# Hybrid decoder trunk on one core: w_down products at other places among the Strassen products, and half of the compression copies on ScalarE

## The chip, the cores and the metric

The kernel runs on one core of a Trainium2 chip. A core has TensorE (matmuls, PE in the profile, and PEld for its weight loads), VectorE (DVE), ScalarE (ACT), GpSimd (POOL) and SyncE (SP, which here only issues transfers). The engines run side by side, each through its own list of instructions in a fixed order, and they wait for one another by semaphores. The metric is the device time of one execution in microseconds (us): 1538.51 us before, the median of 3 runs that lie between 1538.48 and 1538.63.

## The reference: what is computed

Two decoder layers on 512 tokens of width 1024 in float32. A layer normalises its input, projects it with `w_in`, runs two token mixers side by side (forgetting attention with 8 heads; sparse attention with 8 heads whose branches are compressed, selected and sliding-window), gates and mixes them, adds the result to the input, and ends with a squared-ReLU MLP:

```python
kc = compress_blocks(kc, cmp_pos[0], cmp_w1[0], cmp_b1[0], cmp_w2[0], cmp_b2[0])
vc = compress_blocks(vc, cmp_pos[1], cmp_w1[1], cmp_b1[1], cmp_w2[1], cmp_b2[1])
...
x = x + mixed @ w_out
h = rmsnorm(x, norm_mlp)
return x + jnp.square(jax.nn.relu(h @ w_up)) @ w_down
```

`compress_blocks` takes blocks of 32 tokens at a stride of 16 (31 blocks, which overlap by half), adds a position table, and sends each flattened block through two small matrices with a GELU between them. `w_up` is 1024x4096 and `w_down` 4096x1024. A final normalisation follows the second layer.

## The kernel before

**Numbers.** Every large product is made with float32 values split in two: a high half (a cast, `h` or `oh`) and a low half (the value minus the cast, `lo` or `ol`). A block of weights thus costs a cast on ACT and a subtraction on DVE (lines 186 and 187), and one product term costs three matmuls: high by high, high by low, low by high (lines 212, 213, 214).

**Compression.** `compress` (line 498) first lays the tokens of the key `kc` and the value `vc` out anew. For each of the two, two tiles `ca` are filled, one per half of the overlap, each with a memset (506), a copy of the position table (508) and four copies of 64x248 elements (511). That is 16 such copies in a layer, all on DVE. `compress` runs as filler work while the forgetting attention runs; `attend` (469) steps through scores, transposes and values and takes projections and compression between them. In the attention DVE reads the scores out of their bank and finds the row maximum (398, `mx`), ACT makes the exponential (399), PE transposes it into a bank `ps_PT` (421), ACT casts that bank (430, `pth`) and DVE subtracts (431, `ptl`), after which the bank is free for other transposes.

**The MLP.** `w_up` is 32 blocks of 128 columns. The first 8 (`PLAIN`) are plain products. The other 24 are taken in 12 pairs, and each pair is one unit of a Strassen scheme (`unit`, 1228): seven products, here P0 to P6, in place of eight. A Strassen product is 8 matmuls (line 1224): four of 512 columns with the high half of the weights and four of 256 with the low half. P0 goes into a bank `m`; ACT copies it (1245); P1 goes into a bank `p5`, which ACT copies too (1249); P2 is added onto `m`, which ACT copies again (1253); P3 has its own bank (1256); P4 is added onto `m`, and DVE adds the result to both halves of `z` (1260); P5 has its own bank, which DVE reads (1265); P6 is added onto `p5`, which DVE reads (1269). From `z` and then from `y` comes a block of activations each: `act` (1284) runs ReLU, square and a cast on ACT (1289, 1290, 1291) and the low half as a subtraction on POOL (1292). The operands of the next unit are made inside the unit as well (`convert`, 1195): seven casts on ACT, seven subtractions on DVE, and four sums, of which POOL makes two.

There are 32 blocks of activations, numbered 0 to 31: 0 to 7 from the plain products, then two from each unit (unit k, counted from 0, makes 8+2k and 9+2k). Their halves live in the buffers `oh` and `ol`, of which there are eight each, so block j takes the place of block j-8 when all who read that one are done. The tiles `y` and `z` live in four buffers `zz`.

**w_down in the gaps.** The first 24 blocks of activations are consumed in six groups of four. One w_down product takes one group and one of the 8 output blocks: 12 matmuls (lines 212 to 214), with a DVE addition onto the residual `x` behind them (949). That makes 48 products, d0 to d47 here, where d(8c) to d(8c+7) read group c, that is blocks 4c to 4c+3. d0 to d11 come before the units. The other 36 are spread over the 12 units by a list of counts (992). Inside a unit, `between` is called at four places: place 0 between P1 and P2, place 1 between P3 and P4, place 2 between P5 and P6, and place 3 behind P6. A unit with n products puts them at its first n places. With the counts 2, 2, 3, 3, 4, 4, 4, 4, 4, 4, 2, 0, d16 to d18 are in unit 2, d19 to d21 in unit 3, d42 to d45 in unit 9, d46 and d47 in unit 10, and unit 11 has none.

**The last eight blocks.** Activations 24 to 31 are consumed by 8 products of 24 matmuls (one per output block): in layer 0 with 512 columns, in layer 1 (`last`, 1013) in two halves of the tokens with 256 columns, where the seventh of eight terms of two blocks is followed by the eighth of both.

**Order.** The code names an order, but the order on each engine is fixed by a planner when the kernel is built: it takes instructions in the order of the code as far as their inputs and buffers are ready by its own estimate, and lets a later one pass where an earlier one is not. A changed instruction can therefore change the order of those around it. PSUM banks are given out in turn by `bank` (687), two under each of four names, one per product. Weights of w_down come by transfers on SP's queue into one buffer (`crs`) that is refilled when its block is converted; conversion of the next block is asked for inside the current product (`ahead`, 199 and 215).

Of the kernel before, what the change touches and what calls it, by code (L numbers as in the profile page):

```python
# [18 lines left out]
D = 1024  # L19
# [118 lines left out]
def run(*gens):  # L138
    for g in gens:
        for _ in g:  # L140
            pass


class Body:
# [353 lines left out]
    def compress(self, kc, vc, small, l):  # L498

        nc, a = self.nc, self.a  # L500
        A = []
        for x, pos in ((kc, "pos_k"), (vc, "pos_v")):
            t = [self.t("t2", [128, 8, 2, 32], name="ca") for _ in range(2)]
            v = x.rearrange("p (n j r) -> p r j n", j=8, r=2)
            for half in range(2):
                nc.vector.memset(t[half][:, :, 1, 31], 0.0)
                o = OFF[pos] + 8 * half
                nc.vector.tensor_copy(t[half][:, :, 0, 31], small[:, o:o + 8])
                for h in range(2):
                    for r in range(2):  # L510
                        nc.vector.tensor_copy(t[half][r * 64:(r + 1) * 64, :, h, :31],
                                              v[h * 64:(h + 1) * 64, r, :, half:half + 31])
            A.append(t)
            yield
        hp = self.p("O")
# [24 lines left out]
        h = self.t("tmp", [128, 256])  # L540
# [6 lines left out]
        g = self.t("tmp", [128, 4, 64], name="g")  # L547
# [35 lines left out]
        v = self.t("tmp", [128, 2, 64])  # L583
# [344 lines left out]
    def mlp(self, l, x, u, acc, gm):  # L928

        nc, a = self.nc, self.a  # L930
        R = None
        pend = []
        acts = []

        def act(ps):
            t = self.t("tmp", [128, T])
            nc.vector.scalar_tensor_tensor(t, ps, 0.0, R, op0=OP.max, op1=OP.mult)
            h = self.t("oh", [128, T], F32R)
            lo = self.t("ol", [128, T], F32R)
            nc.scalar.activation(t, t, AF.Square)  # L940
            nc.scalar.copy(h, t)
            nc.vector.tensor_tensor(lo, t, h.bitcast(F32), op=OP.subtract)
            acts.append((h, lo))

        def down(c, m, w):

            ps = self.bank()
            yield from self.gemm(ps, w, 4 * (m % 2), acts[4 * c:4 * c + 4], ks=4)
            nc.vector.tensor_add(x[m], x[m], ps)

        def downs():
            for c in range(6):
                for m in range(8):
                    if m % 2 == 0:
                        w = self.weights(a["wd2"][l, c, m // 2])
                    yield lambda: run(down(c, m, w))

        S = Strassen(self, l, x, gm)
        D = downs()
        raws = [None] * 16  # L960
        g0 = self.PLAIN // 2
        S.load(g0)
        for j in range(self.PLAIN):
            ps = self.bank()
            w = self.weights(a["wup"][l, j].rearrange("p k c -> p (k c)"))
            run(self.gemm(ps, w, 0, u))
            if R is None and j == 0:
                pend.append(ps)
                continue
            if R is None:  # L970
                R, _ = self.rstd(acc, (self.turn_tag(), self.turn_tag()))
                prep = S.prepare(R)
                for p in pend:
                    act(p)
            act(ps)
            for _ in range(3):
                next(prep, None)
        conv = S.convert(g0)
        for i in range(12):
            next(D)()  # L980
            if i < 7:
                next(prep, None)
                next(prep, None)
            elif i == 7:
                run(prep)
            else:
                next(conv, None)
                next(conv, None)
            if i == 10:
                S.load(g0 + 1)  # L990
        run(conv)
        for g, n in zip(range(g0, 16), (2, 2, 3, 3, 4, 4, 4, 4, 4, 4, 2, 0)):
            S.load(g + 2)
            S.unit(g, D, n, acts)
        u_next = []
        acts = acts[24:]
        if l + 1 < L:
            acc = []
            self.load_small(l + 1)
            for m in range(8):  # L1000
                ps = self.bank()
                w = self.weights(a["wdn"][l, m].rearrange("p k c -> p (k c)"))
                run(self.gemm(ps, w, 0, acts))
                nc.vector.tensor_add(x[m], x[m], ps)
                acc = self.sumsq(x[m], acc, m == 7)
                u_next.append(self.make_u(x[m], self.gain[:, 16 * l + 16:16 * l + 24], m))
                nc.scalar.dma_start(self.xs[m], x[m])
        else:
            self.last(x, acts, a["wdn"][l])
        self.acc = acc  # L1010
        return u_next
# [106 lines left out]
class Strassen:  # L1118
# [109 lines left out]
    def unit(self, g, D, n, acts):  # L1228
        b, nc = self.b, self.nc
        V, A = nc.vector, nc.scalar  # L1230
        conv = self.convert(g + 1)
        todo = iter(range(n))

        def between():
            if next(todo, None) is not None:
                next(D)()

        def product(i, onto=None):
            ps = b.bank() if onto is None else onto
            self.product(ps, g, i, onto is None)  # L1240
            return ps

        m = product(0)
        y = b.t("zz", [128, 2, 512], name="y")
        A.copy(y[:, 0], m)
        next(conv, None)
        p5 = product(1)
        z = b.t("zz", [128, 2, 512], name="z")
        A.copy(z[:, 1], p5)
        next(conv, None)  # L1250
        between()
        product(2, m)
        A.activation(y[:, 1], m, AF.Copy, scale=-1.0)
        next(conv, None)
        p4 = product(3)
        A.copy(z[:, 0], p4)
        next(conv, None)
        between()
        product(4, m)
        V.tensor_tensor(z, z, m[:, None, :].to_broadcast([128, 2, 512]), op=OP.add)  # L1260
        pair = [None, None]
        self.act(self.halves(z), pair, 0)
        next(conv, None)
        p2 = product(5)
        V.tensor_tensor(y[:, 0], p2, y[:, 0], op=OP.subtract)
        next(conv, None)
        between()
        product(6, p5)
        V.tensor_tensor(y[:, 1], y[:, 1], p5, op=OP.subtract)
        self.act(self.halves(y), pair, 1)  # L1270
        acts += pair
        next(conv, None)
        between()
        for _ in conv:
            pass
# [54 lines left out]
```

## Time and profile before

| what | value |
| --- | --- |
| median of 3 runs | 1538.51 us |
| the profiled execution, its own time | 1538.79 us |
| its span, first to last instruction | 1537.0 us |
| mean granted TensorE clock | 0.998 |
| PE busy | 1516.9 us (99%) |
| DVE busy | 1131.1 us (74%) |
| ACT busy | 808.0 us (53%) |
| POOL busy | 215.5 us (14%) |
| Strassen units of layer 0, of layer 1 | 500.5 to 720.6 us, 1258.2 to 1478.3 us |
| compression copies of layer 0, of layer 1 | from 81.3 us, from 838.9 us |

A row of a timeline gives the start in us, the duration in us, the engine, the line of the kernel, the operation, the tiles (out<-in) with their shapes, and how many instructions the row merges; in brackets behind it stands how long the engine had been idle before it and for whom it waited. Matmuls overlap: one of 512 columns is shown with some 0.40 us, but the next one starts 0.23 us later. Lost time on PE is therefore read from starts, not from durations. In a wait row stand the engine that waited, the instruction it waited for, the total in us, the number of times and the longest. A row of a stretch gives, behind its length, the busy us of PE, PEld, DVE, ACT and POOL.

### The profile page before, as it was taken

Reading aid. Unit: us, or ns where it says so; the run is one execution under the profiler, and the core shown is the slowest. Engines: PE = TensorE matmul, PEld = TensorE weight load, DVE = VectorE, ACT = ScalarE, POOL = GpSimd, SP = SyncE. Lnnn points to the kernel's source line nnn. Section 1 sums busy time; section 2 is a strip of 40 time slices with the busy share of each in tenths; the row PEclk is TensorE's granted clock in tenths of the full one; section 3 lists DMA queues with packets and bytes.
Section 4 is the critical chain, followed back from the end, with each engine's and each line's share of the span. In section 5 each row is a group of like instructions: output and inputs, shape, how many; then the busy total and the mean of one; then the engine's idle time right before and its main releaser. Section 6 shows DMA issues by size and latency. Waiting matters only on the chain.

```text
span 1537.0 us, 21391 instructions
## 1 busy us (share of the span) xinstructions
PE 1516.9 (99%) x7772; PEld 1270.3 (83%) x7772; DVE 1131.1 (74%) x2207; ACT 808.0 (53%) x1513; POOL 215.5 (14%) x178
## 2 busy tenths in 40 slices
PE   9999999999999999999999999999999999999997
PEld 8878888888888888888887788878888887888887
DVE  5588988867479877775646799887574989777753
ACT  6445665553454655555434556555434635655562
POOL 4000000000201332222300000000002023222222
PEclk9999999999999999999999999999999999999999
DMA  7545422143323322322546543222422233223121
GB/s 262 176 127 146 131 69 83 56 128 107 109 85 121 110 96 96 110 83 64 177 142 170 157 120 96 73 79 70 149 98 97 88 118 102 105 95 102 63 97 55
DMA packets 56633, 169.49 MB, mean 110 GB/s; under 512 B 7344, under 2 KB 8112, under 8 KB 56528
## 3 DMA queue, kind: packets, MB, share of 16 engines
q1 hardware_dynamic: 53072, 161.84, 33.2%
q10 hardware_dynamic: 3456, 6.29, 1.2%
q8 instruction: 61, 1.00, 0.3%
q14 instruction: 44, 0.36, 0.1%
HBM read 140.77 MB, written 4.19 MB: 94 GB/s over the span
## 4 chain that ended last, share of the span: by engine, by line
PE 92%; DVE 4%; ACT 1%; DMA 1%; issue 1%; POOL 1%; SPq 0%; DVEq 0%; POOLq 0%; ACTq 0%
PE ps_mm L212 12%; PE ps_mm L213 12%; PE ps_mm L214 12%; PE ps_O L1224 4%; PE ps_S L1224 4%; PE ps_O L447 4%; PE ps_PT L212 3%; PE ps_PT L213 3%; PE ps_PT L214 3%; PE ps_mm L1224 3%; PE ps_PT L1224 3%; PE ps_PT L421 3%; PE ps_S L212 2%; PE ps_S L213 2%; PE ps_S L214 2%; PE ps_O L212 2%
## 5 line engine op out<-in xcount | busy, mean ns | idle before, releaser
L186 ACT CAST wh<-raw 128x1024 fp32r<-128x1024 f32 (+2 forms) x187 | 192.4, 1029 | 254.0 <-PE ps_mm L213 63.1
L187 DVE TENSOR_TENSOR wl<-raw,wh 128x1024 fp32r<-128x1024 f32 (+2 forms) x187 | 227.8, 1218 | 52.4 <-ACT wh L186 51.1
L212 PE MATMUL ps_mm<-uh,wh 128*128 128x512 f32 x512 | 202.4, 395 | 0.0
L213 PE MATMUL ps_mm<-ul,wh 128*128 128x512 f32 x512 | 201.4, 393 | 0.0
L214 PE MATMUL ps_mm<-uh,wl 128*128 128x512 f32 x512 | 201.4, 393 | 0.0
L399 ACT ACTIVATE E<-E,mx 128x128 f32<-128x128 f32 x192 | 107.9, 562 | 75.2 <-DVE mx L398 72.4
L213 PE MATMUL ps_mm<-ol,wh 128*128 128x512 f32 (+1 forms) x324 | 126.1, 389 | 2.7 <-POOL ol L1292 2.7
L212 PE MATMUL ps_mm<-oh,wh 128*128 128x512 f32 (+1 forms) x324 | 126.2, 390 | 0.1
L214 PE MATMUL ps_mm<-oh,wl 128*128 128x512 f32 (+1 forms) x324 | 125.5, 387 | 0.0
L430 ACT CAST pth<-ps_PT 128x512 fp32r<-128x512 f32 x144 | 72.9, 511 | 86.3 <-PE ps_PT L421 86.1
L214 PEld LDWEIGHTS ps_mm<-uh,wl 128*128 128x128 f32 x512 | 96.2, 188 | 19.8
L212 PEld LDWEIGHTS ps_mm<-uh,wh 128*128 128x128 f32 x512 | 96.2, 188 | 18.3 <-ACT E L399 1.5
L1214 DVE TENSOR_TENSOR sl<-s,sh 128x512 fp32r<-128x512 f32 x96 | 85.9, 898 | 31.4 <-ACT sh L1213 30.9
L213 PEld LDWEIGHTS ps_mm<-ul,wh 128*128 128x128 f32 x512 | 96.6, 189 | 14.9
L398 DVE CUSTOM_DVE_ANT_0 E<-ps_S,ct 128x128 f32<-128x128 f32 x192 | 91.5, 480 | 21.6 <-PE ps_S L395 20.4
L431 DVE TENSOR_TENSOR ptl<-ps_PT,pth 128x512 fp32r<-128x512 f32 x144 | 85.3, 595 | 26.1 <-ACT pth L430 25.6
L253 POOL TENSOR_TENSOR acc<-sq 128x512 f32<-128x512 f32 (+1 forms) x6 | 8.6, 1435 | 579.0 <-DVE wl L187 566.0
L421 PE MATMUL ps_PT<-ct,E 128*128 128x128 f32 x480 | 84.3, 274 | 2.5 <-DVE ptl L431 2.5
L1213 ACT CAST sh<-raw 128x512 fp32r<-128x512 f32 x72 | 44.7, 620 | 73.9 <-PE ps_PT L1224 28.1
L1213 ACT CAST sh<-s 128x512 fp32r<-128x512 f32 x96 | 59.4, 619 | 40.3 <-PE ps_O L1224 14.8
L1214 DVE TENSOR_TENSOR sl<-raw,sh 128x512 fp32r<-128x512 f32 x72 | 59.4, 825 | 20.6 <-ACT sh L1213 20.6
L421 PEld LDWEIGHTS ps_PT<-ct,E 128*128 128x128 f32 x480 | 60.1, 140 | 17.1 <-DVE ptl L431 4.2
(420 smaller groups left out, 3948.5 us busy)
## 6 DMA issues: line engine op xcount, KB each, us to landing
raw<-wb SPq DMA_DIRECT2D x64, 512.0 KB, 4.7
raw<-wup SPq DMA_DIRECT2D x64, 512.0 KB, 3.5
raw<-wd SPq DMA_DIRECT2D x48, 512.0 KB, 3.5
kd<-hl SPq DMA_DIRECT2D x48, 256.0 KB, 4.9
w<-w SPq DMA_DIRECT2D x32, 256.0 KB, 4.4
q<-hl SPq DMA_DIRECT2D x64, 128.0 KB, 2.8
raw<-wo SPq DMA_DIRECT2D x16, 512.0 KB, 3.7
raw<-wout SPq DMA_DIRECT2D x16, 512.0 KB, 3.5
```

What stands on the lines that cost most here:

```text
L186: nc.scalar.copy(h[:, :n], raw[:, :n])
L187: nc.vector.tensor_tensor(lo[:, :n], raw[:, :n], h[:, :n].bitcast(F32), op=OP.subtract)
L212: mm(ps, h[:, c], xh, start=start and i == 0, stop=False)
L213: mm(ps, h[:, c], xl, start=False, stop=False)
L214: mm(ps, lo[:, c], xh, start=False, stop=stop and i == ks - 1)
L398: nc.vector.tensor_tensor_reduce(e, ps[:, :n], self.mask[:, T - n:], -1.0, BIG, OP.add, OP.min, mx)
L399: nc.scalar.activation(e, e, AF.Exp, bias=mx, scale=-1.0, accum_out=sm[:, i:i + 1])
L421: nc.tensor.transpose(ps[:, j * 128:(j + 1) * 128], E[i][:, b * 128:(b + 1) * 128], self.ident)
L431: nc.vector.tensor_sub(lo[:, o:o + n], ps[:, :n], h[:, o:o + n].bitcast(F32))
L1213: nc.scalar.copy(h, src)
L1214: nc.vector.tensor_tensor(lo, src, h.bitcast(F32), op=OP.subtract)
L1224: mm = lambda o, w, x, **kw: self.nc.tensor.matmul(o, w, x, skip_group_check=True, **kw)
```

## The change

It has three parts. In `compress`, of each tile's four copies of 64x248 the two that read the upper 64 partitions (`h` = 1) are issued on ACT, the other two stay on DVE: 8 of a layer's 16. In `unit`, the number n of w_down products picks a set of places: for n = 2 places 0 and 1 and for n = 4 all four, as before; for n = 3 places 1, 2 and 3 where it was 0, 1 and 2; for n = 1 place 1. In `mlp`, the counts of the last three units become 3, 1 and 0 where they were 4, 2 and 0, and the two products that are left run behind the last unit. So d16 to d21 and d42 to d44 each stand one place later (d42 to d44 at places 1, 2 and 3 of unit 9), d45 moves from place 3 of unit 9 to place 1 of unit 10, and d46 and d47 move from unit 10 to behind unit 11. The number of matmuls is the same.

```diff
                 for h in range(2):
                     for r in range(2):
-                        nc.vector.tensor_copy(t[half][r * 64:(r + 1) * 64, :, h, :31],
-                                              v[h * 64:(h + 1) * 64, r, :, half:half + 31])
+                        copy = nc.scalar.copy if h else nc.vector.tensor_copy
+                        copy(t[half][r * 64:(r + 1) * 64, :, h, :31], v[h * 64:(h + 1) * 64, r, :, half:half + 31])
...
-        for g, n in zip(range(g0, 16), (2, 2, 3, 3, 4, 4, 4, 4, 4, 4, 2, 0)):
+        for g, n in zip(range(g0, 16), (2, 2, 3, 3, 4, 4, 4, 4, 4, 3, 1, 0)):
             S.load(g + 2)
             S.unit(g, D, n, acts)
+        for d in D:
+            d()
...
-        todo = iter(range(n))
+        places = iter({1: (1,), 2: (0, 1), 3: (1, 2, 3), 4: (0, 1, 2, 3)}.get(n, ()))
+        place = [next(places, None)]
+        here = iter(range(4))
 
         def between():
-            if next(todo, None) is not None:
+            if next(here) == place[0]:
+                place[0] = next(places, None)
                 next(D)()
```

## The prediction

> **What bounds the kernel now.** I read the page first, then PE's waits, then the timelines of the three places where PE stands still.
>
> ```profile
> span 1537.0 us, 21391 instructions
> PE 1516.9 (99%) x7772; PEld 1270.3 (83%) x7772; DVE 1131.1 (74%) x2207; ACT 808.0 (53%) x1513; POOL 215.5 (14%) x178
> ```
>
> TensorE is busy for 1516.9 of 1537.0 us, so nothing that only lightens another engine can pay unless PE waits for that engine. About 20 us are open at most. PE's own waits say where they lie:
>
> ```profile
> PE ps_mm L213 <- POOL ol L1292: 2.7, 2, 1.6
> PE ps_PT L421 <- DVE ptl L431: 2.5, 2, 1.3
> PE ps_S L392 <- DVE mx L398: 1.8, 4, 0.6
> PE ps_PT L213 <- POOL ol L1292: 1.6, 1, 1.6
> ```
>
> Columns: total us, times, longest. These are the four largest. The first and the last are a w_down product (L213) waiting for the low half of an MLP activation; the middle two are the attention stage waiting for DVE. The change touches both kinds.
>
> **Copies: the DVE burst.** The first layer's place on PE, with one row of the second layer, then DVE, then ACT:
>
> ```profile
> 86.87 0.40 PE L214 MATMUL ps_mm<-uh,wl 128*128 128x512 f32 x1
> 88.53 0.55 PE L421 MATMUL ps_PT<-ct,E 128*128 128x128 f32 x3 [1.26 <-DVE ptl L431]
> 89.84 0.40 PE L214 MATMUL ps_mm<-uh,wl 128*128 128x512 f32 x1
> 90.81 0.44 PE L392 MATMUL ps_S<-kd,q 128*128 128x384 f32 x1 [0.57 <-DVE mx L398]
> 91.73 0.40 PE L214 MATMUL ps_mm<-uh,wl 128*128 128x512 f32 x1
> 92.46 0.50 PE L392 MATMUL ps_S<-kd,q 128*128 128x512 f32 x1 [0.33 <-DVE mx L398]
> ...
> 846.09 0.55 PE L421 MATMUL ps_PT<-ct,E 128*128 128x128 f32 x3 [1.26 <-DVE ptl L431]
> ...
> L511 DVE COPY ca<-tmp x32: 352/370/382, 81.3 to 849.1; 64x248 f32<-64x248 f32 x32
> ...
> 85.08 1.53 DVE L511 COPY ca<-tmp 64x248 f32<-64x248 f32 x4
> 87.79 0.68 DVE L431 TENSOR_TENSOR ptl<-ps_PT,pth 128x512 fp32r<-128x512 f32 x1
> 90.48 0.27 DVE L398 CUSTOM_DVE_ANT_0 E<-ps_S,ct 128x128 f32<-128x128 f32 x1
> ...
> 90.86 0.41 ACT L399 ACTIVATE E<-E,mx 128x128 f32<-128x128 f32 x1 [5.00 <-DVE mx L398]
> ...
> 81.00:93.00 12.00, 9.84 (x50) 7.51 (x49) 11.55 (x39) 4.11 (x10) 0.14 (x1) 1.00 0.47 144
> L1173 ACT CAST b<-bs 128x256 fp32r<-128x256 f32 x8 | 3.2, 404 | 1.4 <-DVE bs L1158 1.4
> ```
>
> The stretch row gives busy us of PE, PEld, DVE, ACT, POOL: between 81 and 93 us DVE works 11.55 of 12.00 us and ACT 4.11, and ACT stands still for 5.00 us just before 90.86. A w_down product of twelve 512-column matmuls takes 2.78 us (the rows of the next part), a step of 0.23, so the three halts cost 88.53-86.87-0.23 = 1.43, 0.97-0.23 = 0.74 and 0.73-0.23 = 0.50: 2.67 us. The second layer repeats the first halt to the hundredth; I take 5.3 us in two layers.
>
> The change takes 8 of each layer's 16 copies off DVE: at the 0.38 us of the row of four (1.53/4), 3.06 us. Eight copies run before the subtraction at 87.79; four of them go, 1.5 us against the 1.43 that it is late. Thirteen run before 90.48; six go, 2.3 against 1.43+0.74. All sixteen run before the third halt; 3.06 against 2.67. Each is just covered. What it adds: 8 copies of 248 elements on ACT. No such row exists; the nearest, 128x256, takes 404 ns, so 0.40 each and 3.2 us, in an engine that has 7.9 us free in those 12. What queues behind them on ACT is the exp (L399) and the cast L430, each delayed by at most the copy in hand, 0.4 us. I take 2.4 of 2.67 per layer: **-4.8 us**. Bounds: -5.3, and -2.6 if the copies sit half in the way of the exps.
>
> **w_down products d16 to d21 in units 2 and 3.** I count Strassen units from 0 and w_down products from d0; P0 to P6 are a unit's seven products. d16 is the first to read the activations of unit 1. It moves from between P1 and P2 to between P3 and P4. Rows: a clean product d14 with the start of the P2 behind it and of the P3 behind that; then d16 with P2 in its midst; then what it waits for.
>
> ```profile
> 518.75 0.40 PE L212 MATMUL ps_PT<-oh,wh 128*128 128x512 f32 x1
> 521.53 0.39 PE L1224 MATMUL ps_mm<-t,sh 128*128 128x512 f32 x1
> 522.93 0.40 PE L1224 MATMUL ps_O<-t,sh 128*128 128x512 f32 x1
> 534.18 0.40 PE L212 MATMUL ps_mm<-oh,wh 128*128 128x512 f32 x1
> 539.94 0.50 PE L213 MATMUL ps_mm<-ol,wh 128*128 128x512 f32 x1 [1.61 <-POOL ol L1292]
> 540.51 0.39 PE L1224 MATMUL ps_S<-t,sh 128*128 128x512 f32 x1
> 1297.57 0.50 PE L213 MATMUL ps_PT<-ol,wh 128*128 128x512 f32 x1 [1.61 <-POOL ol L1292]
> ...
> 533.16 0.57 ACT L1245 COPY y<-ps_PT 128x512 f32<-128x512 f32 x1
> 536.71 0.62 ACT L1291 CAST oh<-y 128x512 fp32r<-128x512 f32 x1
> ...
> 538.17 1.71 POOL L1292 TENSOR_TENSOR ol<-y,oh 128x512 fp32r<-128x512 f32 x1
> ```
>
> A clean w_down product is 521.53-518.75 = 2.78 us (12 matmuls at 0.23), a Strassen product 522.93-521.53 = 1.40. d16 and P2 take 540.51-534.18 = 6.33 where 4.18 is due: 2.15 us lost, and the second layer shows the same wait. After the change P2 and P3 fill 534.18 to 536.98, and d16's eleventh matmul, the one that needs the late half, comes at 536.98+10x0.23 = 539.3 against 538.17+1.71 = 539.9. So 0.6 stays and 1.5 goes. P2 and P3 now end earlier, so their two bank copies on ACT can slip ahead of the cast at 536.71; one of 0.57 would leave 1.1 and gain 1.0. I take 1.3 per layer: **-2.6 us**, bounds -2.0 and -4.3. The other moved products read activations at least a unit old; they cost nothing while the cover of rival two holds.
>
> **d45 to d47, and the last pair.** d46 and d47 go behind unit 11. Twelve unchanged matmuls each: no PE time. Their weights come through the same buffers in the same order; SP's fetch and the conversion of the next block stay queued behind d46's start, now 5.5 us before that block is needed. Before, PE went straight on:
>
> ```profile
> 1478.30 0.28 PE L212 MATMUL ps_mm<-oh,wh 128*128 128x256 f32 x1
> 1484.31 0.38 PE L213 MATMUL ps_mm<-ol,wh 128*128 128x256 f32 x1 [1.13 <-POOL ol L1292]
> 1484.53 0.28 PE L214 MATMUL ps_mm<-oh,wl 128*128 128x256 f32 x1
> 1484.65 0.28 PE L213 MATMUL ps_S<-ol,wkd 128*128 128x256 f32 x1
> 1488.37 0.28 PE L212 MATMUL ps_O<-oh,wva 128*128 128x256 f32 x1
> 1482.46 1.79 POOL L1292 TENSOR_TENSOR ol<-z,oh 128x512 fp32r<-128x512 f32 x1 [6.54 <-ACT oh L1291]
> 1484.31 1.29 POOL L1292 TENSOR_TENSOR ol<-y,oh 128x512 fp32r<-128x512 f32 x1
> ...
> 1481.90 1.23 DVE L187 TENSOR_TENSOR wva<-raw,wva 128x1024 fp32r<-128x1024 f32 x1
> ...
> 720.63 0.40 PE L212 MATMUL ps_PT<-oh,wh 128*128 128x512 f32 x1
> 726.23 0.39 PE L212 MATMUL ps_O<-oh,wh 128*128 128x512 f32 x1
> ```
>
> In layer 1, 72 half-width matmuls at 0.12 are 8.64 us, and 1478.30 to 1488.37 is 10.07: 1.43 lost. Layer 0 spends 5.60 on its first 24, against 24x0.23 = 5.5: nothing to win.
>
> The catch is in the buffers. There are eight `oh` and eight `ol`; at the end they hold activations 20 to 27, and d40 to d47 read 20 to 23. Before, d47 ran in unit 10 ahead of P4, so activations 28 to 31 found free buffers. Now those four wait for d47, which is behind unit 11: four casts and four POOL subtractions in a row. If the buffers come free one by one as d47 reads (at -2.1, -1.4, -0.7 and 0 us from its end), the first subtraction starts at -1.2 and, at 1.5 each (between 1.29 and 1.79), they end at +0.3, 1.8, 3.3 and 4.8. Layer 0's next product needs them at +2.9, 3.6, 4.3, 5.0: just met, and I allow 0.3. Layer 1 needs the first three at +1.6, 1.9, 2.3: 1.0 lost in place of 1.43. Together **-0.1 us**. The best is -1.4. The worst: all four come free only at the end and every subtraction takes 1.79, so they end at +2.6, 4.4, 6.2, 8.0; layer 0 then loses 3.0 and layer 1 3.9 in place of 1.43: +5.5.
>
> The subtraction of 1.79 began beside DVE's conversion at 1481.90, that of 1.29 after it had ended. The Trainium skill, page "SBUF — State Buffer", section "Who interferes with whom", says that a DVE instruction with two SBUF inputs contends with a GpSimd instruction that reads SBUF and that the loser waits for the whole instruction. The two rows agree, 0.5 us apart. If by that rule all four subtractions meet conversions of the last weights, they end at +0.6, 2.4, 4.2 and 6.0, layer 0 loses 1.0 and layer 1 1.9, and the sum is 1.6 us higher.
>
> **Sum.** -4.8 - 2.6 - 0.1 = -7.5 us. The profiled execution took 1538.79 us, 1.8 around its span; 1531.3 follows. The median of the runs is 0.28 lower, so 1531.0.
>
> **Rivals.** One: the tail takes the gains back (the worst case above): 1538.5-7.4+5.5 = 1536.6. For it: eight buffers, and POOL's serial rows. Against it: the casts can follow d47's reads singly.
>
> Two, slower: P2 adds onto P0's bank, so it must wait for ACT's copy of it (L1245). A w_down product used to stand between; in units 2, 3, 9 and 10 it no longer does, eight places in two layers. The copy at 533.16 ends at 533.73, only 0.45 before 534.18, where P2 will now stand. If ACT takes the six casts and activations of the last pair first (6x0.6), a place loses up to 3.1. The gain is gone at 0.95 us per place, and 1.3 each makes it slower than before by over 0.2%; at 1.8 each, 1538.5-7.5+14.4 = 1545.4. Against it: unit 11 had no cover before and P2 did not wait there.
>
> Three: the copies gain nothing, because the order of the instructions is planned anew and the ACT copies land before the exps: 1538.5-2.7 = 1535.8. Against it: the 5.00 us of idle ACT.
>
> **Numbers.** Chances: forecast 0.60, rival one 0.15, three 0.15, two 0.10. 0.2% (3.1 us) is about what a measurement of this kernel can tell. The forecast and a third of one and three are faster; the rest of them is same; two is slower, with a little for the new plan: 0.73, 0.16, 0.11. The range goes from all three losses gone, 1538.5-11.0 = 1527.5, to beyond rivals one and three, 1538.
>
> **What would show it.** PE's wait for `ptl` and `mx` at 87 to 92 us gone, with copies of 64x248 on ACT at about 0.40; the wait for `ol` in unit 2 down to 0.6; behind d47, four POOL subtractions in a row. I am wrong if PE waits for an ACT copy ahead of P2, or if L213 waits for `ol` behind d47 by more than 1.5 us per layer.

## The result, and where it came from

The changed kernel takes 1535.05 us (median of 11 runs, 1534.16 to 1536.66) beside 1538.90 for the kernel before in the same session (11 runs, 1537.86 to 1540.33): a ratio of 0.9976, 95% interval 0.9967 to 0.9985. That is 3.85 us faster, where 7.5 were forecast. The profiled execution took 1534.54 us, 2.0 around its span. It is one of the faster of the 11, so the account by stage, below, comes to 4.5 us and not 3.85. Its page and PE's waits (columns: total us, times, longest; the waits left out are under 0.8 or were there before):

```profile
span 1532.5 us, 21386 instructions
PE 1515.8 (99%) x7772; PEld 1270.9 (83%) x7772; DVE 1132.8 (74%) x2191; ACT 816.8 (53%) x1529; POOL 216.8 (14%) x178
...
PE ps_S L392 <- DVE mx L398: 1.2, 2, 0.6
PE ps_S L1226 <- ACT y L1250: 0.9, 2, 0.6
PE ps_O L1226 <- ACT y L1250: 0.9, 2, 0.6
PE ps_mm L213 <- POOL ol L1297: 0.8, 2, 0.6
```

The change shifts line numbers: 1224 is now 1226, 1245 is 1250, 1281 is 1286, 1289 to 1292 are 1294 to 1297, and 511 is 512. Three of the four waits of before look as forecast: `ptl` (2.5) is gone, the waits for `ol` in the units went from 1.6 to 0.5 each (one of them is shown below, at 537.51), the one in the tail from 1.1 to 0.8 in two parts. The fourth, for `mx`, went only from 1.8 to 1.2. Two entries are new, with 1.8 us in four waits: a Strassen product (L1226) waits for ACT's bank copy L1250. This is the wait of rival two.

The starts on PE give the account by stage. From the timeline of before, the first Strassen product of each layer (the prediction shows the other starts of before); then, of after, the same two, the first matmul behind d47 in each layer, and the 73rd from there in layer 1:

```profile
500.51 0.39 PE L1224 MATMUL ps_PT<-b,sh 128*128 128x512 f32 x1
1258.15 0.39 PE L1224 MATMUL ps_mm<-b,sh 128*128 128x512 f32 x1
...
498.07 0.39 PE L1226 MATMUL ps_PT<-b,sh 128*128 128x512 f32 x1
718.39 0.39 PE L212 MATMUL ps_PT<-oh,wh 128*128 128x512 f32 x1
1253.59 0.39 PE L1226 MATMUL ps_mm<-b,sh 128*128 128x512 f32 x1
1473.92 0.28 PE L212 MATMUL ps_mm<-oh,wh 128*128 128x256 f32 x1
1483.88 0.28 PE L212 MATMUL ps_O<-oh,wva 128*128 128x256 f32 x1
```

| stretch | before, us | after, us | difference | forecast |
| --- | --- | --- | --- | --- |
| start to layer 0's units (attention, copies) | 500.51 | 498.07 | -2.44 | -2.4 |
| layer 0's units with their w_down products | 220.12 | 220.32 | +0.20 | -1.3 |
| layer 0's last products to layer 1's units | 537.52 | 535.20 | -2.32 | -2.1 |
| layer 1's units | 220.15 | 220.33 | +0.18 | -1.3 |
| layer 1's tail, 72 matmuls | 10.07 | 9.96 | -0.11 | -0.4 |
| span | 1537.0 | 1532.5 | -4.5 | -7.5 |

The first row holds layer 0's copies, and the third holds layer 1's copies together with layer 0's own last products (+0.3 in the forecast). The moved products brought nothing. The copies brought somewhat less than the first and third rows suggest: in the profile of after, PE is ahead by 0.31 us already at 20 us (a matmul that starts at 20.54 before starts at 20.23), long before the first moved copy at 78.4. Such shifts, from -0.9 to +0.7 us, stand in the first 25 us of all the kernels that follow, so a stage that holds the start is not known better than that.

**The copies.** The lines of the copies, ACT's burst of copies, then the starts on PE around the halt that is left and DVE there, all after:

```profile
L512 ACT COPY ca<-tmp x16: 616/626/651, 78.4 to 842.3; 64x248 f32<-64x248 f32 x16
L512 DVE COPY ca<-tmp x16: 354/366/379, 81.0 to 843.1; 64x248 f32<-64x248 f32 x16
...
84.81 2.58 ACT L512 COPY ca<-tmp 64x248 f32<-64x248 f32 x4
...
86.54 0.40 PE L214 MATMUL ps_mm<-uh,wl 128*128 128x512 f32 x1
89.06 0.44 PE L392 MATMUL ps_S<-kd,q 128*128 128x384 f32 x1 [0.61 <-DVE mx L398]
90.21 0.39 PE L392 MATMUL ps_S<-kd,q 128*128 128x512 f32 x1
...
88.02 0.56 DVE L431 TENSOR_TENSOR ptl<-ps_PT,pth 128x384 fp32r<-128x384 f32 x1
...
88.77 0.23 DVE L398 CUSTOM_DVE_ANT_0 E<-ps_S,ct 128x128 f32<-128x128 f32 x1
```

and one row of DVE before:

```profile
92.32 0.55 DVE L431 TENSOR_TENSOR ptl<-ps_PT,pth 128x384 fp32r<-128x384 f32 x1
```

The matmul ahead of the three halts starts 0.33 us earlier than before (86.54 for 86.87), the score product of the third halt 2.25 earlier (90.21 for 92.46): 1.92 us won at the halts, and 1.93 by the same reading in layer 1. The price on ACT was wrong: 0.626 us instead of 0.40, and four of them stand in a row for 2.58 us. One halt of three survives. It waits for the row maximum at 88.77, and DVE's timeline shows no idle time from 82.7 us to there, so DVE's work sets it and not ACT's burst. All eight copies that DVE kept are done by then, but the plan has put the subtraction of 88.02 and two memsets ahead of the row maximum (0.75 us from 88.02 to 88.77, the length of the halt, 0.78). Before, the row maximum ran at 90.48 and that subtraction behind it, at 92.32. That this order alone makes the halt was not tested.

**What took the moved products' gain back.** PE, DVE and ACT where P2 of unit 3 waits in layer 0; d16's halt in unit 2; then P2 in unit 10:

```profile
549.19 0.40 PE L1226 MATMUL ps_PT<-t,sh 128*128 128x512 f32 x1
551.41 0.50 PE L1226 MATMUL ps_S<-t,sh 128*128 128x512 f32 x1 [0.65 <-ACT y L1250]
552.91 0.39 PE L1226 MATMUL ps_O<-t,sh 128*128 128x512 f32 x1
...
546.28 1.47 DVE L187 TENSOR_TENSOR wl<-raw,wh 128x1024 fp32r<-128x1024 f32 x1 [0.50 <-ACT wh L186]
547.67 0.67 DVE L1274 TENSOR_TENSOR y<-y,ps_O 128x512 f32<-128x512 f32 x1
...
548.87 0.68 DVE L1286 TENSOR_TENSOR y<-y 128x512 f32<-128x512 f32 x1
...
549.59 0.63 ACT L1294 ACTIVATE y<-y 128x512 f32<-128x512 f32 x1 [2.82 <-DVE y L1286]
...
550.79 0.57 ACT L1250 COPY y<-ps_S 128x512 f32<-128x512 f32 x1
...
534.57 0.40 PE L212 MATMUL ps_S<-oh,wh 128*128 128x512 f32 x1
537.51 0.50 PE L213 MATMUL ps_S<-ol,wh 128*128 128x512 f32 x1 [0.49 <-POOL ol L1297]
538.08 0.40 PE L1226 MATMUL ps_PT<-t,sh 128*128 128x512 f32 x1
...
693.51 0.50 PE L1226 MATMUL ps_O<-t,sh 128*128 128x512 f32 x1 [0.22 <-ACT y L1250]
```

d16 now takes 538.08-534.57 = 3.51 us where 2.78 is due: 0.73 lost in place of 2.15, 1.42 won in each layer. In unit 3 the bank of P0 is full when P1 starts at 549.19. But ACT's line has ReLU and square (L1294, L1295) of unit 2's last block ahead of the copy L1250, and ACT has stood idle for 2.82 us until DVE delivers that block. The copy ends at 551.36 and P2 starts at 551.41. P1 and P2 together take 552.91-549.19 = 3.72, where two products of 1.40 are due: 0.9 lost. In unit 9 of layer 0 the plan lets P3 start ahead of P2 (0.42 lost), in unit 10 P2 breaks into P3 and waits 0.22 (0.48 lost, from the starts). Together 1.8 in layer 0, more than the 1.42 won (the table has a balance of +0.20 per layer and not +0.4; the rest, in small steps, was not traced). Units 2 and 11 have no cover either, and P2 does not wait there.

**The tail.** POOL's row of subtractions behind d47 in layer 1, two of DVE's subtractions beside them, and PE's longest wait for them:

```profile
1472.78 2.12 POOL L1297 TENSOR_TENSOR ol<-z,oh 128x512 fp32r<-128x512 f32 x1 [22.94 <-ACT oh L1296]
1474.86 1.28 POOL L1297 TENSOR_TENSOR ol<-y,oh 128x512 fp32r<-128x512 f32 x1
1476.11 1.27 POOL L1297 TENSOR_TENSOR ol<-z,oh 128x512 fp32r<-128x512 f32 x1
1477.34 2.27 POOL L1297 TENSOR_TENSOR ol<-y,oh 128x512 fp32r<-128x512 f32 x1
...
1472.51 1.22 DVE L187 TENSOR_TENSOR wva<-raw,wva 128x1024 fp32r<-128x1024 f32 x1
...
1476.43 2.03 DVE L187 TENSOR_TENSOR wq<-raw,wq 128x1024 fp32r<-128x1024 f32 x1 [1.62 <-ACT wq L186]
...
1477.43 0.38 PE L213 MATMUL ps_mm<-ol,wh 128*128 128x256 f32 x1 [0.60 <-POOL ol L1297]
```

Four in a row, and the first starts 1.1 us before d47 ends at 1473.92, as worked out (1.2). The tail's 72 matmuls take 9.96 us where 8.64 are due: 1.32 lost.

### The profile page after: what moved, and what is told of

It is laid out like the page before. It is cut to its first block, busy times and chain, and to the rows that moved or that the text cites. A ratio compares the mean times of both kernels' runs of the same rounds, so it can differ in the third digit from the quotient of the medians.

```text
span 1532.5 us, 21386 instructions
## 1 busy us (share of the span) xinstructions
PE 1515.8 (99%) x7772; PEld 1270.9 (83%) x7772; DVE 1132.8 (74%) x2191; ACT 816.8 (53%) x1529; POOL 216.8 (14%) x178
## 4 chain that ended last, share of the span: by engine, by line
PE 90%; DVE 4%; ACT 3%; issue 1%; DMA 1%; POOL 1%; SPq 0%; DVEq 0%; ACTq 0%; POOLq 0%
PE ps_mm L212 12%; PE ps_mm L213 12%; PE ps_mm L214 12%; PE ps_S L1226 4%; PE ps_O L1226 4%; PE ps_O L447 4%; PE ps_PT L212 3%; PE ps_PT L214 3%; PE ps_PT L213 3%; PE ps_PT L421 3%; PE ps_PT L1226 3%; PE ps_mm L1226 3%; PE ps_S L213 2%; PE ps_S L214 2%; PE ps_S L212 2%; PE ps_O L213 2%
## 5 line engine op out<-in xcount | busy, mean ns | idle before, releaser
L213 PE MATMUL ps_mm<-ol,wh 128*128 128x512 f32 (+1 forms) x316 | 122.9, 389 | 0.8 <-POOL ol L1297 0.8
L212 PE MATMUL ps_mm<-oh,wh 128*128 128x512 f32 (+1 forms) x316 | 122.9, 389 | 0.1
L214 PE MATMUL ps_mm<-oh,wl 128*128 128x512 f32 (+1 forms) x316 | 122.3, 387 | 0.0
L1216 DVE TENSOR_TENSOR sl<-s,sh 128x512 fp32r<-128x512 f32 x96 | 93.8, 980 | 34.3 <-ACT sh L1215 33.8
```

The source lines that it names most:

```text
L212: mm(ps, h[:, c], xh, start=start and i == 0, stop=False)
L213: mm(ps, h[:, c], xl, start=False, stop=False)
L214: mm(ps, lo[:, c], xh, start=False, stop=stop and i == ks - 1)
L1216: nc.vector.tensor_tensor(lo, src, h.bitcast(F32), op=OP.subtract)
```

## Experiments

The theory at the start: the copies are worth their 4.8, and P2's lost cover (units 3, 9 and 10) eats what d16 wins. The rival: it is the ACT copies, or the new order of ACT's line as a whole, that makes P2 wait. Ratios are against the kernel before, run beside each kernel on the same chip.

**Each half alone.** The ACT copies in the kernel before, and the change with its copies back on DVE:

```diff
-                        nc.vector.tensor_copy(t[half][r * 64:(r + 1) * 64, :, h, :31],
-                                              v[h * 64:(h + 1) * 64, r, :, half:half + 31])
+                        copy = nc.scalar.copy if h else nc.vector.tensor_copy
+                        copy(t[half][r * 64:(r + 1) * 64, :, h, :31], v[h * 64:(h + 1) * 64, r, :, half:half + 31])
```

> The kernel before with only the compression copies of the upper half on ACT. Theory (three separate terms: copies, late d16, second product P2 without cover): 4.7 us faster than before, 1534.2, the PE wait for ptl gone and one wait for mx of 0.8 left per layer, no wait of P2 for ACT's copy of P0's bank. Rival (the new plan of the order is what costs in the Strassen units): waits of P2 for that copy appear here too, in units 3, 9 and 10, and the time stays near 1537.5.

> The changed kernel with all compression copies back on DVE, so the moved w_down products alone. Theory: late d16 gains 1.4 per layer and P2 without cover costs 1.8 per layer, the tail gains 0.2: no gain, 1538.9 to 1539.4. Rival (the losses in units 3, 9 and 10 come from the order planned anew around the ACT copies): they are gone here and 2.5 to 3 us are won, about 1536.

Copies alone: 1534.53 us against 1538.79, ratio 0.9973 (0.9963 to 0.9984), 4.3 us faster, without a wait for the bank copy. Products alone: 1539.34, ratio 1.0003 (0.9994 to 1.0012), no gain, with both waits for L1250 (0.9 each). So the ACT copies have no part in P2's wait, and they alone are the whole gain.

**Cover back, d16 still late.** Each unit gets its places by name; unit 2 takes 1, 2, 3 and unit 3 takes 0, 1, 2, with the ACT copies:

```diff
-        for g, n in zip(range(g0, 16), (2, 2, 3, 3, 4, 4, 4, 4, 4, 4, 2, 0)):
+        for g, n in zip(range(g0, 16), [(0, 1), (0, 1), (1, 2, 3), (0, 1, 2)] + 6 * [(0, 1, 2, 3)] + [(0, 1), ()]):
...
-            if next(todo, None) is not None:
+            if next(here) in n:
```

> Copies on ACT, and of the moved products only those of unit 2 (places 1, 2, 3); unit 3 keeps places 0, 1, 2 and units 9 to 11 keep 4, 2, 0. Theory: the gain of late d16 stays (1.4 per layer) and P2 has its cover in units 3, 9 and 10, so 4.7 + 2.8 = 7.5 us faster than before, 1531.4, which beats the change by 3.6. Rival (cover is not the cause): about the time of the change, 1535.

1531.63 us, ratio 0.9954 (0.9941 to 0.9966): 7.2 us faster than before and 3.4 faster than the change. P2's wait is gone, although ACT's line in unit 3 is the same:

```profile
549.09 0.63 ACT L1291 ACTIVATE y<-y 128x512 f32<-128x512 f32 x1 [2.82 <-DVE y L1283]
...
550.29 0.57 ACT L1247 COPY y<-ps_S 128x512 f32<-128x512 f32 x1
...
552.88 0.39 PE L1226 MATMUL ps_S<-t,sh 128*128 128x512 f32 x1
```

The copy is just as late (it ends at 550.86), but d19, between P1 and P2 again, keeps PE until 552.88 and P2 follows at once.

**Is a lost cover enough?** The kernel before with only unit 3 moved to places 1, 2, 3, and then with unit 2 at 0, 1, 3 as well:

```diff
-        for g, n in zip(range(g0, 16), (2, 2, 3, 3, 4, 4, 4, 4, 4, 4, 2, 0)):
+        for g, n in zip(range(g0, 16), [(0, 1), (0, 1), (0, 1, 2), (1, 2, 3)] + 6 * [(0, 1, 2, 3)] + [(0, 1), ()]):
```

> The kernel before, all copies on DVE, with only unit 3's three products moved from places 0, 1, 2 to 1, 2, 3. Theory: P2 of unit 3 loses its cover and waits some 0.8 for ACT's copy of P0's bank, in both layers: 1.6 to 1.8 us slower than before, 1540.6. Rival (cover is not the cause): within 0.3 us of before.

> The kernel before, all copies on DVE, with unit 2 at places 0, 1, 3 and unit 3 at places 1, 2, 3. Unit 3 without cover alone lost nothing. Theory, amended: P2 waits where it has no cover and the unit before ends with a w_down product at place 3, since then ReLU and square of the last block stand ahead of P0's copy in ACT's line and wait for a DVE subtraction that is late behind the weight conversion. So here PE waits 0.6 to 0.8 for ACT's copy in unit 3 of both layers, 1.6 slower than before, 1540.4. Rival (it takes the late d16, that is the bunching of unit 2, too): no wait for that copy, 1539.1.

1539.09 us, ratio 1.0002 (0.9994 to 1.0011), and 1539.43, ratio 1.0003 (0.9994 to 1.0012). In the first, P2 does not wait, so the theory as it stood was wrong: without cover P2 need not wait. ACT's line in the first of the two, then ACT and PE in the second:

```profile
553.56 0.58 ACT L1247 COPY y<-ps_S 128x512 f32<-128x512 f32 x1
554.04 0.63 ACT L1291 ACTIVATE y<-y 128x512 f32<-128x512 f32 x1
...
553.75 0.57 ACT L1247 COPY y<-ps_S 128x512 f32<-128x512 f32 x1
...
553.97 0.40 PE L1226 MATMUL ps_O<-t,sh 128*128 128x512 f32 x1
554.38 0.50 PE L1226 MATMUL ps_S<-t,sh 128*128 128x512 f32 x1
```

In the first the plan put the copy ahead and the ReLU behind it: the copy ends at 554.14 and P2 starts right behind P1, at 554.32. In the second the ReLU came first again, at 551.25, but after only 0.26 us of waiting for DVE, and the plan let P3 begin ahead of P2. PE's list of waits shows none for the copy there, yet P2 starts at 554.38, just behind the copy that ends at 554.32, and by the starts P2 and P3 take 3.09 us where 2.81 are due. These 0.28 us are lost in each layer, in the way of unit 9 of the change: P3's first matmul hides the wait from the list. So a lost cover costs about the time by which the copy ends behind P2's turn, less what P3 fills: nothing where the copy is 0.18 early, 0.28 where it is 0.35 late (554.32, with P1 done at 553.97), and 0.9 in unit 3 of the change, where it is 0.77 late (551.36, with P1 due to end at 550.59). In the change the copy is that late because a block stands ahead of it on ACT and DVE is late with that block.

**The copy's place in the code.** The second block's ReLU, square and cast are written behind the next unit's first bank copy:

```diff
         A.copy(y[:, 0], m)
+        for f in self.held:
+            f()
+        self.held = []
...
-        self.act(self.halves(y), pair, 1)
-        acts += pair
+        c = self.halves(y)
...
+            def late():
+                self.act(c, pair, 1)
+                acts.extend(pair)
+            self.held = [late]
```

> The changed kernel with the second block's ReLU, square, cast and low half issued in the code behind the next unit's copy of P0's bank, so that ACT takes that copy first. Nothing is left out. Theory (ACT's line, not the missing time): the waits of P2 in units 3, 9 and 10 vanish, 1.8 per layer, the wait of d16 grows by up to 0.5 per layer: 1531.5 to 1532.5. Rival (ACT or DVE has no time left there): the waits stay in another place, about 1535.

1533.78 us, ratio 0.9966 (0.9953 to 0.9978): 1.3 faster than the change, where 2.5 to 3.5 were expected. In unit 9 ACT takes the copy ahead of the block's cast and the loss goes from 0.42 to 0.08; in unit 10 P2 still starts 0.23 late. But in unit 3 ACT kept its old order, ReLU at 549.28 and copy at 550.49: the planner passes an earlier instruction by when it believes the later one's input is ready sooner.

**The late block.** The two low halves of weights that unit 2 asks for are subtracted by POOL, which takes the 1.47 of line 187 out of DVE's line:

```diff
-        nc.vector.tensor_tensor(lo[:, :n], raw[:, :n], h[:, :n].bitcast(F32), op=OP.subtract)
+        eng = nc.gpsimd if self.on_pool else nc.vector
+        eng.tensor_tensor(lo[:, :n], raw[:, :n], h[:, :n].bitcast(F32), op=OP.subtract)
...
+                b.on_pool = g == 6
                 next(D)()
+                b.on_pool = False
```

> The change, with the two low halves of w_down weights that unit 2 asks for subtracted by POOL instead of DVE (two 128x1024 subtractions per layer). Theory: P2 of unit 3 waits because ScalarE's copy of P0's bank stands behind the ReLU and square of unit 2's last block, and that block is late on DVE behind this weight subtraction (1.47 us). Without it on DVE the block is ready 1.4 us sooner (ReLU near 548.2 instead of 549.59), the copy ends before P1 does, and the wait of 0.6 in each layer's unit 3 is gone with the 0.8 to 0.9 that P1 and P2 lost there: 1533.2 to 1533.7, while the waits in units 9 and 10 stay. Rival: the block is late for another reason (P6's end, the subtraction's own order on DVE), or POOL's slower subtraction makes w_down wait for its weights or DVE's two-input work slower beside it: the wait stays and the time is 1535 or more.

1539.48 us, ratio 1.0003 (0.9994 to 1.0011): the gain of the whole change is gone. DVE, POOL, ACT and PE in layer 0's unit 3:

```profile
546.58 2.78 DVE L1218 TENSOR_TENSOR sl<-raw,sh 128x512 fp32r<-128x512 f32 x1 [0.42 <-ACT sh L1217]
...
546.42 2.40 POOL L188 TENSOR_TENSOR wl<-raw,wh 128x1024 fp32r<-128x1024 f32 x1
...
552.37 0.58 ACT L1254 COPY y<-ps_S 128x512 f32<-128x512 f32 x1
...
553.00 0.50 PE L1228 MATMUL ps_S<-t,sh 128*128 128x512 f32 x1 [2.45 <-ACT y L1254]
```

The first subtraction of `y` did come 2.2 us sooner (545.48 for 547.67; this profile is some 0.3 ahead from its start). But the next one on DVE, 0.68 elsewhere, took 2.78 beside POOL's, so the block was 0.4 later than in the change (549.28 for 548.87). With the block's cast and one more cast ahead of it, the copy came 1.6 later, and PE's wait grew from 0.65 to 2.45. Twice 1.8 is 3.6 of the 4.4 us lost. A block that is later, with the copy behind it, thus makes P2's wait longer, and a copy taken ahead of part of the block's work made it shorter in unit 9 above. No run made the block earlier in unit 3. Whether the weights' subtraction alone makes the block late enough is not shown, since this run put another delay in its place.

**The tail.** The last but one pair of blocks goes into two `e` buffers, empty there, instead of `oh` and `ol`:

```diff
-    def act(self, c, pair, i):
+    def act(self, c, pair, i, own=False):
...
+        if own:
+            t = b.t("e", [128, 2, T], F32R, name="eh")
+            h, lo = t[:, 0], t[:, 1]
...
-        self.act(self.halves(z), pair, 0)
+        self.act(self.halves(z), pair, 0, g == 14)
```

> The changed kernel with the two blocks of unit 10 (28 and 29) in two buffers of tag e that stand empty by then, so that they need not wait for d47. Theory (the four casts and POOL subtractions in a row behind d47 are the wait in the tail): layer 1's 1.3 us go, 1533.7, and POOL's subtractions of unit 10 run during unit 11. Rival (the last pair's own chain is what PE waits for, buffers do not matter): the wait stays, 1535.

1533.40 us, ratio 0.9964 (0.9951 to 0.9976), 1.65 faster than the change. The rows in layer 1:

```profile
1461.79 1.30 POOL L1301 TENSOR_TENSOR eh<-z,eh 128x512 fp32r<-128x512 f32 x1 [11.57 <-DVE y L1286]
1465.61 1.30 POOL L1301 TENSOR_TENSOR eh<-y,eh 128x512 fp32r<-128x512 f32 x1 [2.53 <-ACT eh L1300]
```

Two subtractions are done long before they are read, no wait for `ol` is left in the tail, and its 72 matmuls take 8.63 us for 9.96. So the eight buffers were what held them.

**How many copies.** One in four copies on ACT instead of one in two:

```diff
-                        copy = nc.scalar.copy if h else nc.vector.tensor_copy
+                        copy = nc.scalar.copy if h and r else nc.vector.tensor_copy
```

> The change with only one in four compression copies on ScalarE instead of one in two. Theory: the halt of 0.78 per layer that is left in the first attention stage comes from the burst of four ScalarE copies of 0.63 each, which holds up the casts behind it; with two in the burst the casts start about 1.2 sooner and DVE carries two copies more (0.73), so the halt shrinks or goes: 1533.5 to 1535. Rival: what sets the halt is the sum of the copies on DVE, and each copy given back costs about 0.37 there: 1536 to 1538.5.

1537.15 us, ratio 0.9988 (0.9979 to 0.9997): 2.1 slower than the change, 0.26 for each of the 8 copies given back, with the waits for `mx` at 2.0 and for `ptl` at 0.8. The rival is borne out, at 0.26 for a copy where 0.37 was its price: a shorter burst on ACT did not shrink the last halt, which grew (waits of 1.0 for `mx` where 0.6 was), so what stands on DVE ahead of the row maximum sets it. Whether more than half of the copies on ACT would win more was not tried.

**The price of an ACT copy.** Added copies on idle tiles at the start, six forms, four times each:

```diff
+            nc.scalar.copy(qc[:64], pc[:64])
+            nc.scalar.copy(qc[:64], sv[:64, 0, :, :31])
+            nc.scalar.copy(dv[:64, :, 0, :31], pc[:64])
+            nc.scalar.copy(dv[:64, :, 0, :31], sv[:64, 0, :, :31])
+            nc.scalar.copy(qc[:64], pc[64:])
+            nc.scalar.copy(qc, pc)
```

> The kernel before with the ScalarE compression copies and, at its start, four rounds of six ScalarE copies on idle tiles: contiguous 64x248, strided source as in the kernel, strided destination as in the kernel, both, contiguous from the upper 64 partitions to the lower, and contiguous 128x248. Theory: the 0.626 us of a 64x248 compression copy comes from the strided access, on one side or both, so the contiguous ones cost 0.40 or less and the strided ones 0.6. Rival: it is a fixed price of the ScalarE copy or of crossing partitions, and then the contiguous ones, or the crossing one alone, cost 0.6 too. The time itself is about 10 us above that of the kernel with these copies alone at most; only the durations of the added copies are read.

The groups by line (1115 contiguous, 1116 strided source, 1117 strided destination, 1119 from the upper to the lower partitions; the number behind the comma is the mean of one in ns):

```profile
L1116 ACT COPY py<-px 64x248 f32<-64x248 f32 x4 | 2.5, 616 | 0.0
L1119 ACT COPY py<-px 64x248 f32<-64x248 f32 x4 | 1.6, 398 | 0.1
L1117 ACT COPY py<-px 64x248 f32<-64x248 f32 x4 | 1.6, 391 | 0.1
L1115 ACT COPY py<-px 64x248 f32<-64x248 f32 x4 | 1.5, 386 | 0.0
```

Its one run took 1539.55 us. The price comes from the strided source: 616 against 386 ns. Both strides at once (623) cost hardly more than the source's. The strided destination (391), the crossing from the upper to the lower partitions (398) and the full height (382) cost next to nothing.

**Putting it together.** First unit 2 late, all four places of unit 9, one product at place 0 of unit 10, d47 alone behind unit 11, and the `e` buffers; then unit 9 with three products, at 0, 1, 2, so that d46 and d47 stand behind unit 11 (the kernel before has a fourth in unit 9, at place 3):

```diff
-        for g, n in zip(range(g0, 16), (2, 2, 3, 3, 4, 4, 4, 4, 4, 4, 2, 0)):
+        for g, n in zip(range(g0, 16), [(0, 1), (0, 1), (1, 2, 3), (0, 1, 2)] + 5 * [(0, 1, 2, 3)] + [(0, 1, 2), (0,), ()]):
```

> Copies on ACT; unit 2 late (places 1, 2, 3), unit 3 at places 0, 1, 2, unit 9 at all four, unit 10 with d46 at place 0, d47 alone behind unit 11, blocks 28 and 29 in the empty buffers of tag e. Theory: 1.4 less than the kernel with unit 2 late alone (1531.6), since the last wait for the low half in layer 1 goes: 1530.2, 8.6 us faster than before. Rival (the tail's wait is not removed by one product of cover): 1531.6.

> The compression copies shared as in the change, unit 2 at places 1, 2, 3, unit 3 at 0, 1, 2, unit 9 at 0, 1, 2 as in the kernel before, unit 10 with one product at place 0, two products behind unit 11, and the last but one pair of blocks in two empty e buffers. Theory: the w_down products of units 2 and 3 give 1.4 per layer and the copies 2.2 per layer, as in the kernel with unit 2 late (1531.63), and with two products of cover behind unit 11 the layer 1 wait of 1.3 for POOL's last subtraction shrinks to 0.6 or less while the buffers keep the subtractions from queueing: 1530 to 1531. Rival: it is only traded, because the last subtraction is set by unit 11's own chain on DVE and POOL, and one more product behind unit 11 is one less inside: 1531.4 to 1532, with the wait for POOL still above 1.0.

The first: 1531.39 us, ratio 0.9951 (0.9938 to 0.9963), the same as with unit 2 late alone; layer 1 still waits 1.3 for POOL: one product behind unit 11 is too little cover for the last block. The second: 1530.25, ratio 0.9941 (0.9928 to 0.9955), 8.8 us faster than before and the fastest of all; no wait for `ol` is left in the tail and none for the bank copy.

## Why the prediction was half right

The time fell, and it lies inside the range, but the gain was 3.85 us where 7.5 were forecast. By its steps:

- **Copies, -4.8: the mechanism was right, the size too large.** The copies alone brought 4.3. The three halts lay where the DVE rows put them, and they gave 1.92 and 1.93 (2.67-0.78 = 1.89 by the halts themselves), not 2.4. That the stages show -2.44 and -2.3, close to the forecast, is in part luck: 0.33 of the first stands ahead of the halts and came with the start, and 0.1 to 0.2 more in small steps behind them. Two prices were off. An ACT copy costs 0.626 us, not the 0.40 of a contiguous 128x256 row, and what the casts behind them can be delayed by is a burst of 2.58 us, not one copy of 0.4. The halt of 0.78 per layer that is left, though, stands where the prediction counted only copies ahead of DVE's row maximum: the new plan also put a subtraction and two memsets there, so the wait for `mx` was not gone.
- **d16, -2.6: the halt itself was right, the term was not.** 0.73 was left of 2.15 where 0.6 was worked out, and 1.42 per layer was won. The step that failed is the sentence behind it: "The other moved products read activations at least a unit old; they cost nothing while the cover of rival two holds." The cover did not hold. Giving up the product between P1 and P2 in unit 3 cost 0.9, in units 9 and 10 0.42 and 0.48, and the term came out at +0.4 instead of -2.6. These 3.0 us are most of the 3.65 that are missing.
- **Rival two was the right mechanism at too low a chance and too high a price.** It had named the wait, the instruction and the eight places. The evidence held against it, that P2 does not wait in unit 11, was weak: unit 11 never waited in any of these kernels, and units 3, 9 and 10 did. It had also named what makes it costly, ACT taking the last block's work before the copy; what it lacked is that DVE can be late with that block. A lost cover is free when ACT reaches the copy in time (1539.09 us with unit 3 bare); it costs when the plan has put a block before the copy, most where DVE is late with that block. Its price was 0.4 to 0.9 at three places per layer, not 1.8 at four.
- **The tail, -0.1: right in the sum, in part by luck.** Four subtractions follow each other as drawn. Layer 1 lost 1.32 where 1.0 was worked out, so it won 0.11 and not 0.4; layer 0 lost nothing where 0.3 was allowed (its first 24 matmuls take 5.52 in place of 5.60). The two misses cancel. The 2.12 and 2.27 of the first and last subtraction, each beside a DVE subtraction (1472.51 and 1476.43), show the contention with DVE's conversions that the Trainium skill's page "SBUF — State Buffer" states in "Who interferes with whom" (1.28 without it). DVE's subtraction of 1476.43, begun beside one of POOL's, takes 2.03 for 1.22. PE's waits in the tail are still only 0.8 in all.

Rival three, that the copies gain nothing, fell with the first stage. Rival one's mechanism was there but cost nothing net: the time was given back in the units, not in the tail. Two of the prediction's numbers don't follow from its own working: 1.3 us at eight places less 7.5 is 2.9, not over 0.2%; and the forecast with a third of rivals one and three is 0.70, not 0.73.

## What to carry to other kernels

When a product is moved away from between two others, price what it had been covering: look up, on the engine that has to read the bank in between, which instruction stands ahead of that read and how late its input is. A list of waits can hide such a loss where another product's matmul fills the gap; the starts show it. Move the late consumers alone and leave the rest where they give cover: with only unit 2's products moved, and unit 3's first one left between P1 and P2, the gain is 7.2 us in place of 3.85. And a price for a moved copy is taken from a row with the same access pattern, not only the same size.

## What the runs showed of the hardware

An ACT copy of 64x248 floats whose source steps by 64 bytes takes 616 to 626 ns, 230 more than a contiguous one, while a destination in eight pieces costs 5 ns. The Trainium skill's page "SBUF — State Buffer" says, in "Door 1: The DMA port swizzle (why `[64,N]` ≈ `[32,N]`)", that an access which crosses to a new 16-byte line pays a penalty; the rows agree for this source, at 0.93 ns an element more; no other step was tried. DVE reads the same source in 366 ns; what it would take contiguous, no run here shows.

Two subtractions with both inputs in SBUF, on DVE and POOL at once, nearly run one after the other: 2.78 for 0.68 us on DVE beside POOL's 2.40. Work handed to POOL to relieve DVE cost DVE 2.1 us and gave it back 1.47.
